# A two-layer transformer on one core: norm weights folded into an output weight, rotary tables made earlier, first loads issued from two queues

## The chip, the core and the metric

One core of one Trainium2 chip runs the whole program. The metric is the device time of one execution in microseconds; a kernel's time is the median of several executions. The engines are TensorE (PE, matmuls), VectorE (DVE), ScalarE (ACT), GpSimd (POOL) and SyncE (SP, which issues most transfers).

## The reference

Two layers over 256 positions of width 1024, all in float32. Layer 0 has a gated linear attention (GLA), layer 1 a block attention with rotary embedding, and each is followed by a gated feed-forward network (FFN). The lines that the change touches:

```python
def rms_norm(x, g, eps=1e-6):
    xf = x.astype(jnp.float32)
    return (xf * lax.rsqrt(jnp.mean(xf * xf, -1, keepdims=True) + eps) * g).astype(x.dtype)

def gla_mixer(x, w_in, w_gk, b_gk, norm_g, w_out):
    q, k, v, g, gk_low = split_cols(x @ w_in, GLA_COLS)
...
    o = from_heads(rms_norm(o.astype(x.dtype), norm_g)) * jax.nn.silu(g)
    return o @ w_out

def partial_rope(x, positions):
    inv_freq = ROPE_THETA ** (-jnp.arange(0, ROPE_DIM, 2, dtype=jnp.float32) / ROPE_DIM)
    ang = positions.astype(jnp.float32)[:, None, :, None] * inv_freq
    cos, sin = jnp.cos(ang), jnp.sin(ang)
...
```

`norm_g` has 256 weights, one for each column of a head; the four heads use the same ones. `cos` and `sin` depend on the positions alone and are first used in layer 1.

## The kernel before

**Products in three passes.** A float32 matrix is split into a rounded part `h` and the rest `l`, both in a format that TensorE runs at full rate, and each product is three matmuls: hh, lh and hl (`mm3`, L291 to L293). So every weight of 128x1024 elements costs an ACT cast (`h`, L263) and a DVE subtraction (`l`, L264) after its 512 KB load; activations are transposed on TensorE (`transpose_split`, L306) and split in the same way (L315 on ACT, L319 on DVE).

**The order is planned when the program is built.** Every step is an `Op` with an engine, a cost from a formula and its reads and writes. `Plan.emit` is a list scheduler: it takes the engine and the step that can start first by these costs, among equals the one created first (steps marked `urgent` may go ahead), and writes the instructions out in that order. Each engine then runs its instructions strictly in that order and waits at each for what it needs. The costs are guesses: for DVE 0.14 us + 0.97 ns for each element of a row, for a load its KB / 330 on SP and 2.3 us more until it lands. Large tiles share 41 slots of 128x1024 elements, given out in order of creation; a load whose slot isn't free yet holds SP.

**The start.** DVE zeroes a tile, and PE multiplies it with itself 7 times (`busy(WARM[0])`, L670; each is two instructions in the trace). SP issues `ident`, the two halves of x's first 128 rows (`x0`), the first two 256 KB pieces of the V weights (`wv00`, `split2`, L273 to L276), the halves of `x1`, then 512 KB pieces of weights. x is transposed into `xT0`; the V product (tile `v`) follows.

**The first attention.** V's first half, the decay chain (`gk`, `pre`, then Abs, Exp, Ln, a scan and three Exp, L728 to L766), K and Q (`gk`, `gq`), scores (`sc`, L819), V's second half, and then for each 128 rows `t`: the attention products (`o`, L862), the sums of squares (L871), the gate product `g` in two blocks with Silu (`sg`, L844), the multiplication of `sg` with `normg` on POOL (L848), and `og`, the product of `o`, the norm factor and `sg` on DVE (L887). `og` is transposed (`trg`, L896) and split (L900, L904), and `out_proj` multiplies it with `gla_w_out` (tile `y`, weights `wo0` to `wo7`).

**The rotary tables** (`rope_tables`, L920 to L950) are created after that projection: three small loads, then 18 DVE instructions on 32x256 elements and two ACT Sin. Their planned costs are 0.637 + 4 x 1.013 + 0.388 = 5.08 us of DVE. They are first used in layer 1. The FFN of layer 0 follows (tiles `fg`, `fu`, `d`, `A`, `X`).

Of the kernel before, what the change touches and what calls it, by code (L numbers as in the profile page):

```python
# [37 lines left out]
WARM = (7, 4)  # L38
# [153 lines left out]
def kernel(ctx, tc, x, positions, gla_w_in, gla_w_gk, gla_b_gk, gla_norm_g, gla_w_out,  # L192
# [30 lines left out]
    normg = fixed("normg", (P, GLA_DV))  # L223
# [60 lines left out]
    def w_row(name, w, k):  # L284
        return split(name, lambda raw: [(raw, w[k * P:(k + 1) * P, :])])
# [634 lines left out]
    def rope_tables():  # L920
        dma(lambda: nc.sync.dma_start(rcol.f, c_f32[:, 2 * P:2 * P + 2]), 4, [], [rcol])
        dma(lambda: nc.sync.dma_start(cmask.f, c_f32[:, P:2 * P]), 64, [], [cmask])
        dma(lambda: nc.sync.dma_start(q32(posb).bitcast(I32), positions[0:1, :].broadcast_to([ROPE, S])), 32,
            [], [posb])

# [187 lines left out]
```

## Time and profile before

| what | value |
|---|---|
| executions timed | 588.75, 591.04, 591.47 us |
| median | 591.04 us |
| the profiled execution, its own time | 588.38 us |
| its span (first to last instruction) | 586.6 us |
| granted TensorE clock, mean | 0.997 |
| PE / PEld / DVE / ACT / POOL busy | 97 / 83 / 86 / 58 / 7% of the span |

The profiled execution lies 1.78 us above its span and 2.66 us under the median. PE's busy time contains the junk matmuls of the start.

### The profile page before, as it was taken

Reading aid. Unit: us, or ns where it says so; the run is one execution under the profiler, and the core shown is the slowest. Engines: PE = TensorE matmul, PEld = TensorE weight load, DVE = VectorE, ACT = ScalarE, POOL = GpSimd, SP = SyncE. Lnnn points to the kernel's source line nnn. Section 1 sums busy time; section 2 is a strip of 40 time slices with the busy share of each in tenths; the row PEclk is TensorE's granted clock in tenths of the full one; section 3 lists DMA queues with packets and bytes.
Section 4 is the critical chain, followed back from the end, with each engine's and each line's share of the span. In section 5 each row is a group of like instructions: output and inputs, shape, how many; then the busy total and the mean of one; then the engine's idle time right before and its main releaser. Section 6 shows DMA issues by size and latency. Waiting matters only on the chain.

```text
span 586.6 us, 8058 instructions
## 1 busy us (share of the span) xinstructions
PE 571.8 (97%) x3006; PEld 488.0 (83%) x3006; DVE 506.3 (86%) x627; ACT 340.1 (58%) x452; POOL 42.8 (7%) x43
## 2 busy tenths in 40 slices
PE   8999998999999999999999999999999999999994
PEld 7899886888878887889889999888887888888983
DVE  4889169988999999999895689988989999999826
ACT  4893455254948586776364356634585767677310
POOL 1022211010010101000000000000101000010001
PEclk9999999999999999999999999999999999999998
DMA  8985176248687878887375545626767888988201
GB/s 267 381 297 166 67 257 208 91 165 232 218 228 231 237 217 284 205 304 251 104 252 187 158 130 188 218 91 215 173 222 226 206 260 204 299 204 275 84 0 72
DMA packets 56233, 118.43 MB, mean 202 GB/s; under 512 B 4945, under 2 KB 9585, under 8 KB 56194
## 3 DMA queue, kind: packets, MB, share of 16 engines
q1 hardware_dynamic: 51842, 109.53, 56.4%
q0 software_dynamic: 4352, 8.39, 8.4%
q8 instruction: 23, 0.38, 0.2%
q14 instruction: 16, 0.13, 0.1%
HBM read 116.85 MB, written 1.05 MB: 201 GB/s over the span
## 4 chain that ended last, share of the span: by engine, by line
PE 83%; DVE 9%; DMA 4%; issue 2%; ACT 0%; SPq 0%; DVEq 0%; ACTq 0%
PE fy L293 6%; PE fy L291 6%; PE fy L292 6%; PE pa L544 4%; PE pa L543 4%; PE pa L541 4%; PE tr L306 3%; PE v L293 3%; PE v L291 3%; PE v L292 3%; DMA d0r<-in_ffn_w_down 2%; PE y L292 2%; PE y L293 2%; PE y L291 2%; PE pc L544 2%; PE pc L543 2%
## 5 line engine op out<-in xcount | busy, mean ns | idle before, releaser
L561 DVE TENSOR_TENSOR A<-A,X 128x1024 f32<-128x1024 f32 x48 | 57.2, 1214 | 0.0
L567 POOL DMA_DIRECT2D X<-in_ffn_w_gu x16 | 19.5, 1236 | 205.5 <-DVE e L595 61.8
L315 ACT CAST xT<-tr 128x512 fp32r<-128x512 f32 x16 | 9.3, 589 | 34.5 <-PE tr L306 34.4
L362 POOL TENSOR_TENSOR st<-st,mhalf 128x1 f32<-128x1 f32 x8 | 7.6, 955 | 252.9 <-DVE st L360 252.9
L499 ACT CAST C0h<-X 128x1024 fp32r<-128x1024 f32 x8 | 8.4, 1053 | 10.9 <-DMA X<-in_ffn_w_gu 10.9
L350 DVE SCALAR_TENSOR_TENSOR r<-xn,fy 128x512 f32<-128x512 f32 x8 | 5.5, 684 | 9.6 <-PE fy L293 9.6
L306 PE MATMUL tr<-ident,e 128*128 128x128 f32 x64 | 9.7, 274 | 2.8 <-DVE e L595 2.7
L306 PEld LDWEIGHTS tr<-ident,e 128*128 128x128 f32 x64 | 7.6, 140 | 5.7 <-issue 4.3
L499 ACT CAST D0h<-A 128x1024 fp32r<-128x1024 f32 x8 | 8.4, 1051 | 6.6 <-DVE A L561 6.6
L499 ACT CAST C1h<-X 128x1024 fp32r<-128x1024 f32 x8 | 8.4, 1051 | 5.9 <-DMA X<-in_ffn_w_gu 5.9
L354 DVE BATCH_NORM_STATS2 st<-r 128x6 f32<-128x512 f32 x16 | 11.1, 693 | 0.5
L319 DVE TENSOR_TENSOR xT<-tr,xT 128x512 fp32r<-128x512 f32 x16 | 10.8, 683 | 0.6 <-ACT x32b L326 0.6
L499 ACT CAST A1h<-A 128x1024 fp32r<-128x1024 f32 x8 | 8.4, 1051 | 5.0 <-DMA A<-in_ffn_w_gu 5.0
L372 DVE SCALAR_TENSOR_TENSOR xn<-r,st,lnb 128x512 f32<-128x512 f32 x16 | 11.3, 745 | 0.0
L499 ACT CAST A0h<-A 128x1024 fp32r<-128x1024 f32 x8 | 8.4, 1055 | 4.8 <-DMA A<-in_ffn_w_gu 4.7
L368 DVE SCALAR_TENSOR_TENSOR r<-r,st,lng 128x512 f32<-128x512 f32 x16 | 11.2, 744 | 0.0
L499 ACT CAST B1h<-A 128x1024 fp32r<-128x1024 f32 x8 | 8.4, 1054 | 3.5 <-DVE A L561 3.3
L499 ACT CAST B0h<-A 128x1024 fp32r<-128x1024 f32 x8 | 8.4, 1050 | 2.7 <-DVE A L561 2.7
L499 ACT CAST G1h<-A 128x1024 fp32r<-128x1024 f32 x8 | 8.4, 1054 | 2.5 <-DVE A L561 2.2
L500 DVE TENSOR_TENSOR G0l<-A,G0h 128x1024 fp32r<-128x1024 f32 x8 | 9.7, 1215 | 0.1
L500 DVE TENSOR_TENSOR E0l<-X,E0h 128x1024 fp32r<-128x1024 f32 x8 | 9.7, 1216 | 0.0
L500 DVE TENSOR_TENSOR D0l<-A,D0h 128x1024 fp32r<-128x1024 f32 x8 | 9.7, 1216 | 0.0
(1034 smaller groups left out, 2269.3 us busy)
## 6 DMA issues: line engine op xcount, KB each, us to landing
X<-in_ffn_w_gu SPq DMA_DIRECT2D x48, 512.0 KB, 5.0
A<-in_ffn_w_gu SPq DMA_DIRECT2D x16, 512.0 KB, 4.3
X<-in_ffn_w_gu POOLq DMA_DIRECT2D x16, 512.0 KB, 8.6
lng<-in_ln_g SPq DMA_DIRECT2D x4, 512.0 KB, 3.6
lnb<-in_ln_b SPq DMA_DIRECT2D x4, 512.0 KB, 5.3
x<-in_x SPq DMA_DIRECT2D x4, 256.0 KB, 4.5
fg00r<-in_ffn_w_gu SPq DMA_DIRECT2D x2, 512.0 KB, 6.5
fg01r<-in_ffn_w_gu SPq DMA_DIRECT2D x2, 512.0 KB, 7.3
```

What stands on the lines that cost most here:

```text
L291: nc.tensor.matmul(ps, lh, rh, start=start, stop=False)
L292: nc.tensor.matmul(ps, ll, rh, start=False, stop=False)
L293: nc.tensor.matmul(ps, lh, rl, start=False, stop=stop)
L306: nc.tensor.transpose(ps.f[:, j * P:(j + 1) * P], src.f[:, k * P:(k + 1) * P], ident.f)
L372: nc.vector.scalar_tensor_tensor(out=xn.f[:, sl], in0=r.f[:, sl], scalar=st.f[:, 15:16], in1=b.f[:, sl], op0=ALU.mult, op1=ALU.add)
L499: act(1024, lambda: nc.scalar.copy(hi.r, raw.f), [raw], [hi])
L500: dve(1024, lambda: nc.vector.tensor_tensor(out=lo.r, in0=raw.f, in1=hi.f, op=ALU.subtract), [raw, hi], [lo])
L541: nc.tensor.matmul(ps.f, sh, wh.r[:, cs], start=first and q == 0 and j == 0, stop=False, skip_group_check=True)
L543: nc.tensor.matmul(ps.f, sl_, wh.r[:, cs], start=False, stop=False, skip_group_check=True)
L544: nc.tensor.matmul(ps.f, sh, wl.r[:, cs], start=False, stop=last_ and q == 1 and j == 1, skip_group_check=True)
L561: dve(1024, lambda q=q, other=other: nc.vector.tensor_tensor(out=raws[q].f, in0=raws[q].f, in1=other.f, op=ALU.add), [raws[q], other], [ra ...
L567: nc.gpsimd.dma_start(uv(raws[q]), unit(kh, gu, q, c0), accum_op=ALU.add)
```

## The change

- The multiplication of `sg` with `normg` on POOL is gone. `normg` is now loaded as two columns of 128 values, and the split of `gla_w_out` multiplies each row by its weight: ACT's cast takes it as a scale, DVE's subtraction becomes a multiply and subtract.
- `rope_tables` is created before the loads of V's second half. Its four tiles take slots there, and its steps come earlier in the order of creation.
- `ident` and the two pieces of `wv00` are issued from ACT; x from SP, with `x0`'s first half first. An empty step of 0.8 us on SP exists in the plan alone.
- `wv00` and `wv01` are loaded in two halves each, and their casts go to ACT instead of DVE. The second junk block has 3 matmuls instead of 4 and stands between the two halves of x0's transposes.

The moved rotary code is the same text in both places and is cut here.

```diff
--- before.py
+++ after.py
@@ -35,7 +35,7 @@
 SLOTS = 41
 BANKS = {"acc": 4, "ps": 4}
 HOLD = {"PE": 0.0, "DVE": 0.5, "ACT": 0.5, "POOL": 0.0, "SP": 0.0}
-WARM = (7, 4)
+WARM = (7, 3)
 
 
 class Buf:
@@ -220,7 +220,7 @@
     cmask = fixed("cmask", (P, P))
     imask = fixed("imask", (P, P), I32)
     rcol = fixed("rcol", (P, 2))
-    normg = fixed("normg", (P, GLA_DV))
+    normg = fixed("normg", (P, GLA_DV // P))
     wgk = fixed("wgk", (GLA_RANK + 1, 512))
     gkT = fixed("gkT", (GLA_RANK + 1, S))
     rope = fixed("rope", (ROPE, 2, S))
@@ -250,7 +250,8 @@
         return pl.op("POOL", 1.3, fn, reads, writes, extra=8.0, **kw)
 
 
-    def split(name, parts, zero=False):
+    def split(name, parts, zero=False, scale=None):
+
         raw, hi, lo = S_(name + "r"), S_(name + "h", True), S_(name + "l", True)
         if zero:
             gps(500, lambda: nc.gpsimd.memset(raw.f, 0.0), [], [raw])
@@ -260,29 +261,38 @@
             for dst, src in parts(raw.f):
                 nc.sync.dma_start(dst, src)
         dma(load, kb, [], [raw])
-        act(1024, lambda: nc.scalar.copy(hi.r, raw.f), [raw], [hi])
-        dve(1024, lambda: nc.vector.tensor_tensor(out=lo.r, in0=raw.f, in1=hi.f, op=ALU.subtract), [raw, hi], [lo])
+        if scale is None:
+            act(1024, lambda: nc.scalar.copy(hi.r, raw.f), [raw], [hi])
+            dve(1024, lambda: nc.vector.tensor_tensor(out=lo.r, in0=raw.f, in1=hi.f, op=ALU.subtract), [raw, hi], [lo])
+        else:
+            act(1024, lambda: nc.scalar.activation(hi.r, raw.f, AF.Copy, scale=scale[1]), [raw, scale[0]], [hi])
+            dve(1024, lambda: nc.vector.scalar_tensor_tensor(out=lo.r, in0=raw.f, scalar=scale[1], in1=hi.f,
+                                                             op0=ALU.mult, op1=ALU.subtract), [raw, hi, scale[0]], [lo])
         return hi, lo
 
-    def split2(name, w, k0, c0):
+    def split2(name, w, k0, c0, act_queue=False):
         raw, hi, lo = S_(name + "r"), S_(name + "h", True), S_(name + "l", True)
         hi.fine = True
         for j in range(2):
             sl = slice(512 * j, 512 * j + 512)
             k = k0 + j
-            dma(lambda sl=sl, k=k: nc.sync.dma_start(raw.f[:, sl], w[k * P:(k + 1) * P, c0:c0 + 512]), 256,
-                [], [(raw, j)])
-            dve(512, lambda sl=sl: nc.vector.tensor_copy(hi.r[:, sl], raw.f[:, sl]), [(raw, j)], [(hi, j)], fast=True, urgent=True, prio=-1)
+            if act_queue:
+                pl.op("ACT", 0.45, lambda sl=sl, k=k: nc.scalar.dma_start(
+                    raw.f[:, sl], w[k * P:(k + 1) * P, c0:c0 + 512]), [], [(raw, j)], extra=3.6 + 1.3 * j, urgent=True)
+            else:
+                dma(lambda sl=sl, k=k: nc.sync.dma_start(raw.f[:, sl], w[k * P:(k + 1) * P, c0:c0 + 512]), 256,
+                    [], [(raw, j)])
+            act(512, lambda sl=sl: nc.scalar.copy(hi.r[:, sl], raw.f[:, sl]), [(raw, j)], [(hi, j)], urgent=True)
             dve(512, lambda sl=sl: nc.vector.tensor_tensor(out=lo.r[:, sl], in0=raw.f[:, sl], in1=hi.f[:, sl],
-                                                           op=ALU.subtract), [(raw, j), (hi, j)], [(lo, j)])
+                                                           op=ALU.subtract), [(raw, j), (hi, j)], [(lo, j)], urgent=True)
         return hi, lo
 
     def w_kcols(name, w, k0, nk, c0, n):
         src = w[k0 * P:(k0 + nk) * P, c0:c0 + n].rearrange("(k p) c -> p k c", p=P)
         return split(name, lambda raw: [(raw.rearrange("p (k c) -> p k c", k=nk), src)])
 
-    def w_row(name, w, k):
-        return split(name, lambda raw: [(raw, w[k * P:(k + 1) * P, :])])
+    def w_row(name, w, k, scale=None):
+        return split(name, lambda raw: [(raw, w[k * P:(k + 1) * P, :])], scale=scale)
 
     def load_cols(name, w, c0):
         return [w_kcols(f"{name}{i}", w, 2 * i, 2, c0, 512) for i in range(KT // 2)]
@@ -416,8 +426,8 @@
         sl = slice(512 * blk, 512 * blk + 512)
         act(512, lambda: nc.scalar.copy(vt[t].f[:, sl], ps.f), [ps], [(vt[t], blk)])
 
-    def out_proj(aT, w, xo, gb, dstT, keep):
-        ws = [w_row(f"wo{k}", w, k) for k in range(KT)]
+    def out_proj(aT, w, xo, gb, dstT, keep, scale=None):
+        ws = [w_row(f"wo{k}", w, k, scale and scale(k)) for k in range(KT)]
         xn = []
         for t in range(2):
             y = [pl.buf("acc", f"y{t}{hf}") for hf in range(2)]
@@ -671,13 +681,12 @@
         return f
     pl.op("PE", 2.9, busy(WARM[0]), [zeros], [junkps])
     xs = [S_("x0"), S_("x1")]
-    dma(lambda: nc.sync.dma_start(ident.f, c_f32[:, 0:P]), 64, [], [ident])
-
-    def load_x(t):
-        for hf in range(2):
-            sl = slice(512 * hf, 512 * hf + 512)
-            dma(lambda xt=xs[t], t=t, sl=sl: nc.sync.dma_start(xt.f[:, sl], x[t * P:(t + 1) * P, sl]), 256,
-                [], [(xs[t], hf)])
+    pl.op("ACT", 0.45, lambda: nc.scalar.dma_start(ident.f, c_f32[:, 0:P]), [], [ident], extra=2.8, urgent=True)
+
+    def load_x(t, hf, extra):
+        sl = slice(512 * hf, 512 * hf + 512)
+        pl.op("SP", 0.78, lambda xt=xs[t]: nc.sync.dma_start(xt.f[:, sl], x[t * P:(t + 1) * P, sl]), [], [(xs[t], hf)],
+              extra=extra)
 
     def keyed(T, fn):
         T.keys = fn
@@ -688,20 +697,23 @@
         return keyed(T, lambda t, k: Tk(T, t, k))
 
     T0 = new_xT("xT0")
-    load_x(0)
-    for hf in range(2):
-        transpose_split(xs[0], T0, 0, hf, skey=hf)
-    pl.op("PE", 1.0, busy(WARM[1]), [zeros, xs[0]], [junkps], urgent=True)
-
+    load_x(0, 0, 2.9)
 
     w0 = gla_w_in[0]
     V0, G0, GK0 = 1024, 2048, 3072
     v_sb = [S_("v0"), S_("v1")]
-    wv0 = [split2("wv00", w0, 0, V0)]
-    load_x(1)
+    wv0 = [split2("wv00", w0, 0, V0, True)]
+    pl.op("SP", 0.8, lambda: None)
+    load_x(0, 1, 2.9)
     for hf in range(2):
+        transpose_split(xs[0], T0, 0, hf, skey=hf)
+        if hf == 0:
+            pl.op("PE", 0.6, busy(WARM[1]), [zeros, (xs[0], 0)], [junkps], urgent=True)
+    for hf in range(2):
+        load_x(1, hf, 2.9)
         transpose_split(xs[1], T0, 1, hf, skey=hf)
-    wv0 += [w_kcols(f"wv0{i}", w0, 2 * i, 2, V0, 512) for i in range(1, KT // 2)]
+    wv0.append(split2("wv01", w0, 2, V0))
+    wv0 += [w_kcols(f"wv0{i}", w0, 2 * i, 2, V0, 512) for i in range(2, KT // 2)]
     vps = [pl.buf("acc", f"v0{t}") for t in range(2)]
     for i in range(KT // 2):
         for t in range(2):
@@ -803,7 +815,8 @@
     gps(350, lambda: nc.gpsimd.tensor_copy(kxv()[:, 1, :, 0:CHUNK], ch(qd, 2)), [qd], [(kx, 3)])
 
     dma(lambda: nc.sync.dma_start(imask.f, c_i32), 64, [], [imask])
-    dma(lambda: nc.sync.dma_start(normg.f, gla_norm_g[0:1, :].broadcast_to([P, GLA_DV])), 128, [], [normg])
+    dma(lambda: nc.sync.dma_start(normg.f, gla_norm_g[0].rearrange("(c p) -> p c", p=P),
+                                  ), 8, [], [normg])
     scs = [S_("sc0"), S_("scx")]
 
     def scv(i):
@@ -830,6 +843,45 @@
     pe(4 * 512, fscx, [kx], [psx])
     act(512, lambda: nc.scalar.copy(scv(2), psx.f.rearrange("p (h c) -> p h c", h=GLA_H)), [psx], [(scs[1], 0)])
 
+
+    posb, ang, kk_, rr_ = S_("posb"), S_("ang"), S_("kk"), S_("rr")
+
+    def q32(b):
+        return b.f[0:ROPE, 0:S]
+
+    def rope_tables():
+        dma(lambda: nc.sync.dma_start(rcol.f, c_f32[:, 2 * P:2 * P + 2]), 4, [], [rcol])
+        dma(lambda: nc.sync.dma_start(cmask.f, c_f32[:, P:2 * P]), 64, [], [cmask])
+        dma(lambda: nc.sync.dma_start(q32(posb).bitcast(I32), positions[0:1, :].broadcast_to([ROPE, S])), 32,
+            [], [posb])
+
...
+    rope_tables()
     wv1 = load_cols("wv1", w0, V0 + 512)
     v_block(1, 0, T0, wv1, v_sb)
 
@@ -842,11 +894,6 @@
         act_block(ps, T0, ws, t)
         sl = slice(512 * blk, 512 * blk + 512)
         act(512, lambda: nc.scalar.activation(sg[t].f[:, sl], ps.f, AF.Silu), [ps], [(sg[t], blk)], table="silu")
-
-        def fg():
-            v3 = sg[t].f[:, sl].rearrange("p (j c) -> p j c", j=2)
-            nc.gpsimd.tensor_tensor(out=v3, in0=v3, in1=normg.f.unsqueeze(1).broadcast_to([P, 2, GLA_DV]), op=ALU.mult)
-        gps(512, fg, [(sg[t], blk), normg], [(sg[t], blk)])
 
     wgs = [load_cols("wg0", w0, G0), load_cols("wg1", w0, G0 + 512)]
     for t in range(2):
@@ -909,49 +956,10 @@
     gb = load_ln(0, 0)
     T1 = new_xT("xT1")
     x32 = [S_("x32a"), S_("x32b")]
-    xs = out_proj(ogT, gla_w_out[0], xs, gb, T1, x32)
-
-
-    posb, ang, kk_, rr_ = S_("posb"), S_("ang"), S_("kk"), S_("rr")
-
-    def q32(b):
-        return b.f[0:ROPE, 0:S]
-
...
+    xs = out_proj(ogT, gla_w_out[0], xs, gb, T1, x32, lambda k: (normg, normg.f[:, k % 2:k % 2 + 1]))
 
     gb = load_ln(0, 1)
     T2 = new_xT("xT2")
-    rope_tables()
     xs = ffn(0, xs, T1, gb, T2, False, x32)
```

## Rows read from the trace of the kernel before

**Rows 1.** Busy time of each engine by stretch; PE, PEld, DVE, ACT, POOL, clock, DMA.

```profile
0.00:4.60 4.60, 3.36 (x15) 3.10 (x15) 0.43 (x3) 1.28 (x1) 2.17 (x7) 1.00 0.50 133
4.60:9.70 5.10, 3.96 (x24) 3.56 (x25) 2.61 (x6) 1.63 (x3) 0.00 (x0) 1.00 0.94 311
9.70:96.90 87.20, 87.20 (x513) 76.81 (x511) 64.17 (x77) 56.66 (x78) 13.49 (x12) 1.00 0.71 246
96.90:99.00 2.10, 0.04 (x1) 0.03 (x1) 2.10 (x4) 0.53 (x1) 0.00 (x0) 1.00 0.00 0
140.00:560.00 420.00, 417.23 (x2176) 355.13 (x2176) 386.03 (x463) 260.45 (x342) 20.69 (x18) 1.00 0.69 208
```

**Rows 2.** Who waited for whom, PE: us in total, times, longest.

```profile
PE tr L306 <- DVE e L595: 2.7, 3, 1.4
PE trg L896 <- DVE og L887: 2.1, 1, 2.1
```

**Rows 3.** Timeline of the start: start, us, what; in brackets the idle time before.

```profile
0.74 0.38 SPq L674 DMA_DIRECT2D ident<-in_c_f  x1
1.18 0.89 SPq L679 DMA_DIRECT2D x<-in_x  x2
3.06 0.91 SPq L679 DMA_DIRECT2D x<-in_x  x2
...
4.60 1.94 PE L306 MATMUL tr<-ident,x 128*128 128x128 f32 x8 [0.18 <-DMA x<-in_x]
...
8.54 1.41 PE L306 MATMUL tr<-ident,x 128*128 128x128 f32 x8 [1.02 <-DMA x<-in_x]
...
9.71 0.48 PE L291 MATMUL v<-wv00h,xT 128*128 128x512 f32 x1
```

**Rows 4.** Instructions of tile x and of tile wv00r: issue to landing.

```profile
DMA to landing us min/median/max: 3.3/4.5/5.6
...
DMA to landing us min/median/max: 5.2/5.2/5.2
```

**Rows 5.** Timeline of the stage of the stall, 87 to 99 us.

```profile
87.66 1.41 DVE L927 CAST ang<-posb 32x256 f32<-32x256 int32 x1 [2.46 <-DMA posb<-in_positions]
...
94.49 0.58 ACT L844 ACTIVATE sg<-g 128x512 f32<-128x512 f32 x1
...
95.15 1.31 POOL L848 TENSOR_TENSOR sg<-sg,normg 128x512 f32<-128x512 f32 x1 [6.23 <-ACT sg L844]
95.26 1.47 DVE L936 SCALAR_TENSOR_TENSOR rr<-kk,ang 32x256 f32<-32x256 f32 x1
...
98.39 0.85 DVE L887 SCALAR_TENSOR_TENSOR og<-o,ss,sg 128x256 f32<-128x256 f32 x2
99.00 0.74 PE L896 MATMUL trg<-ident,og 128*128 128x128 f32 x4 [2.07 <-DVE og L887]
```

**Rows 6.** Instructions of tile kk alone, 82 to 104 us: DVE busy, count.

```profile
82.00:104.00 22.00, 5.20 (x12) 1.00 0.64 217
```

**Rows 7.** Busy time by stretch of the first attention, columns as in rows 1.

```profile
20.00:36.00 16.00, 16.00 (x123) 15.19 (x122) 12.61 (x12) 14.43 (x17) 0.00 (x0) 1.00 1.06 381
36.00:48.00 12.00, 12.00 (x102) 12.00 (x102) 12.00 (x14) 11.15 (x12) 4.94 (x5) 1.00 0.56 194
58.00:68.00 10.00, 10.00 (x46) 8.27 (x45) 0.36 (x2) 5.08 (x12) 2.19 (x2) 1.00 0.17 54
```

**Rows 8.** Timeline before the scores, and the first score matmuls (tile sc, first to last).

```profile
44.32 1.39 POOL L800 COPY kx<-ke 128x256 f32<-128x256 f32 x1
...
49.58 0.68 DVE L781 SCALAR_TENSOR_TENSOR qd<-gq,ep 128x512 f32<-128x512 f32 x1
...
L819 PE MATMUL sc<-qd,ka x16: 217/275/275, 51.5 to 54.7; 128*128 128x64 f32 x16
```

**Rows 9.** Timeline of ACT in the decay chain.

```profile
29.18 1.28 ACT L749 ACT_TABLE_LOAD   x1
30.47 1.06 ACT L749 ACTIVATE la<-la 128x1024 f32<-128x1024 f32 x1
```

More of the change, by code (lines that the diff above doesn't have):

```diff
@@ L831, with f0, f1, f2 @@
     act(512, lambda: nc.scalar.copy(scv(2), psx.f.rearrange("p (h c) -> p h c", h=GLA_H)), [psx], [(scs[1], 0)])
+    posb, ang, kk_, rr_ = S_("posb"), S_("ang"), S_("kk"), S_("rr")
[6 more added lines that the diff above has]
+            [], [posb])
+        def f0():
+            nc.vector.tensor_copy(q32(ang), q32(posb).bitcast(I32))
+            nc.vector.tensor_scalar_mul(q32(ang), q32(ang), rcol.f[0:ROPE, 0:1])
+        dve(512, f0, [posb, rcol], [ang])
+        for which, off in ((0, 0.25), (1, 0.0)):
+            def f1(off=off, which=which):
+                k_, r_, a_ = q32(kk_), q32(rr_), q32(ang)
+                nc.vector.tensor_scalar(out=k_, in0=a_, scalar1=1.0 / TWO_PI, scalar2=off, op0=ALU.mult, op1=ALU.add)
+                nc.vector.tensor_scalar_add(k_, k_, MAGIC)
+                nc.vector.tensor_scalar_add(k_, k_, -MAGIC)
+                nc.vector.scalar_tensor_tensor(out=r_, in0=k_, scalar=-C1, in1=a_, op0=ALU.mult, op1=ALU.add)
+            def f2(which=which):
+                k_, r_ = q32(kk_), q32(rr_)
+                nc.vector.scalar_tensor_tensor(out=r_, in0=k_, scalar=-C2, in1=r_, op0=ALU.mult, op1=ALU.add)
+                nc.vector.scalar_tensor_tensor(out=r_, in0=k_, scalar=-C3, in1=r_, op0=ALU.mult, op1=ALU.add)
+                if which == 0:
+                    nc.vector.tensor_scalar_add(r_, r_, math.pi / 2.0)
+                nc.vector.tensor_scalar(out=r_, in0=r_, scalar1=SIN_MAX, scalar2=-SIN_MAX, op0=ALU.min, op1=ALU.max)
+            dve(900, f1, [ang], [kk_, rr_])
+            dve(900, f2, [kk_, rr_], [rr_])
+            act(256, lambda which=which: nc.scalar.activation(rope.f[:, which, :], q32(rr_), AF.Sin), [rr_],
+                [(rope, which)], table="silu")
+        dve(256, lambda: nc.vector.tensor_scalar_mul(rope.f[:, 1, :], rope.f[:, 1, :], rcol.f[0:ROPE, 1:2]),
+            [(rope, 1), rcol], [(rope, 1)])
+    rope_tables()
     wv1 = load_cols("wv1", w0, V0 + 512)
@@ L911 @@
     x32 = [S_("x32a"), S_("x32b")]
-    xs = out_proj(ogT, gla_w_out[0], xs, gb, T1, x32)
-    posb, ang, kk_, rr_ = S_("posb"), S_("ang"), S_("kk"), S_("rr")
-    def q32(b):
-        return b.f[0:ROPE, 0:S]
[L920 to L924, printed above, removed]
-        def f0():
-            nc.vector.tensor_copy(q32(ang), q32(posb).bitcast(I32))
-            nc.vector.tensor_scalar_mul(q32(ang), q32(ang), rcol.f[0:ROPE, 0:1])
-        dve(512, f0, [posb, rcol], [ang])
-        for which, off in ((0, 0.25), (1, 0.0)):
-            def f1(off=off, which=which):
-                k_, r_, a_ = q32(kk_), q32(rr_), q32(ang)
-                nc.vector.tensor_scalar(out=k_, in0=a_, scalar1=1.0 / TWO_PI, scalar2=off, op0=ALU.mult, op1=ALU.add)
-                nc.vector.tensor_scalar_add(k_, k_, MAGIC)
-                nc.vector.tensor_scalar_add(k_, k_, -MAGIC)
-                nc.vector.scalar_tensor_tensor(out=r_, in0=k_, scalar=-C1, in1=a_, op0=ALU.mult, op1=ALU.add)
-            def f2(which=which):
-                k_, r_ = q32(kk_), q32(rr_)
-                nc.vector.scalar_tensor_tensor(out=r_, in0=k_, scalar=-C2, in1=r_, op0=ALU.mult, op1=ALU.add)
-                nc.vector.scalar_tensor_tensor(out=r_, in0=k_, scalar=-C3, in1=r_, op0=ALU.mult, op1=ALU.add)
-                if which == 0:
-                    nc.vector.tensor_scalar_add(r_, r_, math.pi / 2.0)
-                nc.vector.tensor_scalar(out=r_, in0=r_, scalar1=SIN_MAX, scalar2=-SIN_MAX, op0=ALU.min, op1=ALU.max)
-            dve(900, f1, [ang], [kk_, rr_])
-            dve(900, f2, [kk_, rr_], [rr_])
-            act(256, lambda which=which: nc.scalar.activation(rope.f[:, which, :], q32(rr_), AF.Sin), [rr_],
-                [(rope, which)], table="silu")
-        dve(256, lambda: nc.vector.tensor_scalar_mul(rope.f[:, 1, :], rope.f[:, 1, :], rcol.f[0:ROPE, 1:2]),
-            [(rope, 1), rcol], [(rope, 1)])
```

## The prediction

> **What bounds the kernel now.** I read the table of busy time by stretch first [rows 1]: from 9.70 to 96.90 us TensorE is busy without a break, and from 140 to 560 it lacks 420 - 417.23 = 2.77 us. The span is TensorE's work plus the few places where it has none. Two such places lie where the change works: the start, in which the first useful product begins at 9.71 us [rows 3], and 96.90 to 99.00, in which PE is busy 0.04 of 2.10 us [rows 1]. The list of waits gives that second one its name, 2.1 us for `og` on VectorE, and shows that the only other long PE wait is 2.7 us in three pieces in the FFNs [rows 2]. Cheaper ScalarE or GpSimd work elsewhere is worth nothing; a change is worth what it takes from these holes, less what it opens elsewhere.
>
> **The stall at 97 us.** The timeline shows why `og` is late [rows 5]. VectorE begins the rotary tables at 87.66, and its in-order queue runs them between the splits and `og`. The twelve instructions on `kk` take 5.20 us [rows 6], the cast of the positions 1.41 [rows 5], and five more of the same 32x256 shape some 0.3 each: about 8.1 us. The plan gave the tables 5.08 us. So VectorE runs about 3.0 us behind the plan by which `trg` was placed in PE's queue, and PE pays 2.07 [rows 5]. Part of the 3.0 is one instruction of 1.47 us which runs beside the POOL multiplication of `sg` (95.15 for 1.31 us) [rows 5]; the other eleven on `kk` average (5.20 - 1.47) / 11 = 0.34, so undisturbed it would be about 1.1 shorter, and the tables about 7.0.
>
> The change takes both out of this stage. `sg` is ready at 94.49 + 0.58 = 95.07; without the POOL step `og` needn't wait until 95.15 + 1.31 = 96.46, and without the tables VectorE is 7 to 8 us ahead. `og` could then start right after `sg`, at about 95.1, take 0.85, and `trg` follow at about 96.2, before PE has run out at 96.90; ACT, which also waited for VectorE's sines in front of `sg`, only gets earlier. I take the whole 2.07. Bounds: 0 if a new plan places `trg` just as tightly, 2.07 the whole hole.
>
> **The POOL step and the scaled split.** The four POOL multiplications lie beside full PE work except in that last one, so they give nothing more. The scaled subtraction of `gla_w_out` on DVE is of another kind of instruction (three operands); the nearest rows, 0.68 for `qd` with 512 elements [rows 8] and 0.85 for the two `og` [rows 5], show nothing dearer than a plain subtraction by more than a tenth. Eight times 0.1 to 0.2 is 0.8 to 1.6 us of DVE, and DVE is busy only 0.36 of 10 us from 58 to 68 [rows 7], where most of them run: cost 0. Without that cover it would be late for `y`, at 0.8.
>
> **The start.** PE's order is: transposes of x0, junk, transposes of x1, then `v`. `v` starts at 9.71 because x1's second half came last: the x1 transposes wait 1.02 us for x at 8.54 [rows 3]. SP issues x1 fourth, from 3.06 for 0.91, so its second half at about 3.5; issue to landing is 5.6 at most [rows 4]: 9.1. After the change SP begins with x: x1's second half is the fourth issue on SP instead of the seventh, at 0.74 + 3 x 0.45 = 2.1, 1.4 earlier. But latency grows along the queue, 3.3 to 5.6 us [rows 4], so the bytes wait for the DMA engines, not for the issue; and ahead of x1's last half lie the same bytes as before, since `wv00` now comes from ACT at the same time. On that view only the head of the queue is gained, the 0.44 between `ident` and x (0.74 and 1.18 [rows 3]). So 0.44 to 1.4. From 0 to 4.60 us the DMA share is 0.50 and from 4.60 to 9.70 0.94 at 311 GB/s, against 1.06 at 381 later [rows 1, 7], so there is a little room for a second queue, and I take 0.6. It reaches the end undiminished, since PE has no other break before 96.90.
>
> The Trainium skill speaks against the second queue ("DMA: Bandwidth & Descriptors", section "Issuing engines are not separate DMA queues"): transfers of all issuing engines end on the same 16 DMA engines, and a second issuer saves only the issue time. By it the start gives 0.44 instead of 0.6, and the sum below 2.5 instead of 2.7; the growing latencies agree with it.
>
> `wv00` and `wv01` are cast by ACT (0.59 for 512 columns as in the `sg` row of 0.58 [rows 5]) instead of DVE; ACT is busy 1.63 of 5.10 us then [rows 1], so this is hidden behind x1's landing. If ACT's first table load stood ahead of its issues, `ident` and `wv00` would be issued 1.28 later [rows 9]; `wv00` then at 2.0 + 0.4 = 2.4 lands by 5.2 [rows 4] at 7.6, still before x1: 0. The junk block that is one matmul shorter lies in PE's wait for x, the empty SP step issues nothing, and `normg`, now 256 single values, is needed first by the split of `wo0` after 50 us: 0 each.
>
> **The tables in their new place.** Created before V's second half, they come when their positions land, at 20 to 36 us. VectorE has 16 - 12.61 = 3.39 us free there, and from 36 to 48 none [rows 7]; the rest of 7.0 pushes the splits of `wv1` and `wg` back by 3.6 us, into the free time from 58 to 68 [rows 7]. Queued behind them are `qd` and `kx`, and behind these the scores on PE. The second `qd` ends at 49.58 + 0.68 = 50.26, the scores begin at 51.5 [rows 8]: slack 1.2. The plan's error moves too, 7.0 - 5.08 = 1.9; it costs PE 1.9 - 1.2 = 0.7 if nothing absorbs it and nothing if the 3.39 us free before it do. I take 0, and keep 0 and 2.8 (two more us of wait for a landing that comes late in a full queue) as bounds. Four slots less, SP issues four weight loads later; `wg` has some 10 us in hand (the free stretch [rows 7]): 0, and without that some 1.4 us for each late load (512 KB at 381 GB/s [rows 7]).
>
> **The sum.** 2.07 + 0.6 - 0 = 2.7 us less. Against the profiled execution: span 586.6 - 2.7 = 583.9, and with the 1.78 around it 585.7. That execution lies at the low end: 588.38, and the three runs 588.75, 591.04, 591.47. The mean of the four is 589.9, and I count from there: 589.9 - 2.7 = **587.2**. Less than 0.5% (about 3 us) either way can't be told from no change.
>
> **The rivals.**
> A, the sum as above: 587.2 (586.2 to 588.4).
> B, more is gained: the first product isn't queued behind x1. `wv00`, issued at 1.2, lands by 5.2 [rows 4] at 6.4; cast, subtraction and hand-overs (0.59 + 0.68 + 0.4) make 8.0, so `v` starts 1.7 earlier, not 0.6; and with 7 us less on VectorE ahead of the FFN the longest wait there, 1.4 [rows 2], may go. 2.07 + 1.7 + (0 to 1.4) = 3.8 to 5.2: 584.7 to 586.1. For it: VectorE is behind in that stretch. Against it: the 1.4 comes 70 us later, and the order of PE at the start is x1 first.
> C, the stall moves: VectorE is behind the plan by 2 to 4 us at `qd`, and PE waits 0.7 to 2.8 for the scores. 2.7 - 0.7 = 2.0 to 2.7 - 2.8 = -0.1: 587.9 to 590.0. For it: the mechanism is that of the stall removed, and VectorE is full there.
> D, slower: the Sin stand in ACT's in-order queue amid Exp and Ln, wait for positions and tables, and hold the decay chain, whose last copy on POOL before the scores ends at 44.32 + 1.39 = 45.71, 5.8 ahead of them [rows 8]. It decides from a delay of 5.8 + 2.7 = 8.5 us on. All DVE work of the tables (8.1) and two more table loads of 1.28 [rows 9] make 10.7: PE would wait 4.9, net 2.2 slower, 592.1; with a late landing of another 2 us 594.1. Against it: the chain's steps are urgent and were created first.
> Of the loads the skill says more ("ScalarE: Activation LUTs", section "What ACT_TABLE_LOAD costs"): 2.66 us for a switch, a drain included. The trace shows 1.28 with the next step 0.01 later [rows 9]; by the page D's two loads would be 5.3 and its time 594.8.
>
> **How the numbers follow.** A 0.40, B 0.22, C 0.25, D 0.13. B and about half of A lie more than 0.5% below, with a little of C from the runs' own spread: faster 0.45. Half of A, nearly all of C and a quarter of D are within: same 0.45. The rest of D: slower 0.10. The range reaches from just under B's lower end, 584.3, over C to the first half of D, 591.2, and leaves out D's dearer half and some of the runs' spread; A alone gives 586.2 to 588.4.
>
> **What would show it.** Right: no PE hole between the last `g` and `y`; the rotary instructions among the splits at 25 to 40 us; no POOL work on `sg`; `v` at about 9.1; `sc` follows its neighbours without a gap. Wrong: a PE wait at `sc` on `qd` (C) or on `kb` (D), a hole of 1 us or more at another `trg` or in the FFN from the new order, or `v` at or after 9.7. If `v` starts before the x1 transposes it is B. The clock was granted in full, 1.00, from 4.60 us on [rows 1]; if it isn't when `v` begins, the new place of the junk has cost that.

## The result, and the profile after

The changed kernel takes 586.69 us (median of 9 executions, 585.54 to 589.76) beside 590.73 for the kernel before (9 executions, 588.41 to 592.05): a ratio of 0.9942, 95% interval 0.992 to 0.9963. It is faster by 0.58%, and its time lies 0.5 us from the 587.2 predicted. The gain fits less well: 4.0 us between these medians, 2.7 predicted; the prediction counted from 589.9, and the kernel before took 590.73 here. In the experiments below the changed kernel was timed once more: 0.9958, 0.9939 to 0.9978, a gain of 3.2. The profiled execution after took 585.54 us with a span of 583.8, against 588.38 and 586.6, and this pair has a gain of 2.8. Executions of one kernel differ with the mean granted clock: of 31 of the kernel before (those timed beside the first four experiments), the five at 0.990 to 0.991 took 592.2 to 593.7 us and the eight at 0.997 to 0.998 587.7 to 590.8.

"Lead" below means how much earlier a matmul starts than the same matmul of the kernel before. Read from the two timelines of PE, the lead is 1.65 us at the first `v` (8.06 against 9.71 [rows 3]), 1.70 at the first `sc`, 0.55 at the first `y`, 2.93 at the first matmul of `y` with `wo7`, 3.17 at the first `y` of layer 1, and 2.8 in the span. So the path to 2.8 was not the predicted one: more was won at the start, something was lost again at the scores, and the hole at 97 us gave a little more than was expected. (The list of waits counts from the modelled end of the matmul before; counted in starts, a hole is 0.1 to 0.3 us longer.)

Timeline of the start after the change (start, us, what; in brackets the idle time before it):

```profile
0.74 0.41 ACTq L684 DMA_DIRECT2D ident<-in_c_f  x1
0.74 1.80 SPq L688 DMA_DIRECT2D x<-in_x  x4
1.17 0.93 ACTq L280 DMA_DIRECT2D wv00r<-in_gla_w_in  x2
2.14 1.28 ACT L285 ACT_TABLE_LOAD   x1 [2.14 <-issue]
...
7.67 0.63 PE L316 MATMUL tr<-ident,x 128*128 128x128 f32 x4 [0.32 <-DMA x<-in_x]
...
8.06 0.48 PE L301 MATMUL v<-wv00h,xT 128*128 128x512 f32 x1
```

All four halves of x are now issued by 2.54 us; before, the last went out at about 3.5 [rows 3]. The order on PE is unchanged: `v` still follows the transposes of x1.

Timeline at the scores, and the list of PE's waits:

```profile
49.06 0.67 DVE L793 SCALAR_TENSOR_TENSOR qd<-gq,ep 128x512 f32<-128x512 f32 x1
49.66 1.20 DVE L266 TENSOR_TENSOR wg01l<-wg01r,wg01h 128x1024 fp32r<-128x1024 f32 x1
50.80 0.67 DVE L793 SCALAR_TENSOR_TENSOR qd<-gq,ep 128x512 f32<-128x512 f32 x1
...
51.52 0.43 PE L832 MATMUL sc<-qd,ka 128*128 128x64 f32 x2 [0.63 <-DVE qd L793]
```

```profile
PE tr L316 <- DVE e L605: 2.0, 3, 0.8
...
PE sc L832 <- DVE qd L793: 0.6, 1, 0.6
```

This is a new wait. PE came to the scores 1.70 us earlier, and VectorE finished the second `qd` at 50.80 + 0.67 = 51.47 instead of 50.26 [rows 8]. The matmuls that need it would have begun at about 50.73. Between `sc` and the next V product the lead falls from 1.70 to 0.60, 0.8 of it (from 50.73 to 51.52) at the recorded wait of 0.63. Some 0.2 more goes at the last score product (`scx`, which needs `kx`): it starts at 54.39, right behind POOL's copy into `kx`:

```profile
42.67 6.73 POOL L812 COPY kx<-ke 128x256 f32<-128x256 f32 x1
51.53 2.81 POOL L815 COPY kx<-qd 128x256 f32<-128x256 f32 x1 [2.13 <-DVE qd L793]
```

The second copy ends at 54.34. Before, these two copies took 1.39 [rows 8] and 1.33.

Timeline of the former stall, and busy time from 97 to 99 us (columns as in rows 1):

```profile
93.23 0.58 ACT L896 ACTIVATE sg<-g 128x512 f32<-128x512 f32 x1
...
95.50 0.47 DVE L934 SCALAR_TENSOR_TENSOR og<-o,ss,sg 128x256 f32<-128x256 f32 x1
...
96.22 0.60 PE L943 MATMUL trg<-ident,og 128*128 128x128 f32 x4
```

```profile
97.00:99.00 2.00, 2.00 (x11) 1.59 (x10) 2.00 (x3) 1.79 (x3) 0.00 (x0) 1.00 0.00 0
```

`og` is done in time, `trg` starts with no idle time before it, and PE is busy 2.00 of 2.00 us, where it was busy 0.04 of 2.10 [rows 1, 5].

The tables run where they were expected, from 29.08 on, and ScalarE's part of them shows the additional table loads:

```profile
30.67 1.28 ACT L879 ACT_TABLE_LOAD   x1
32.68 0.42 ACT L879 ACTIVATE rope<-rr 32x256 f32<-32x256 f32 x1 [0.73 <-DVE rr L876]
33.01 1.03 ACT L265 CAST wv10h<-wv10r 128x1024 fp32r<-128x1024 f32 x1
34.05 1.28 ACT L776 ACT_TABLE_LOAD   x1
36.21 1.06 ACT L776 ACTIVATE em<-cum 128x1024 f32<-128x1024 f32 x1 [0.87 <-DVE cum L764]
```

After each of these loads ScalarE still waits for VectorE (0.73 and 0.87 us). PE never waits for the decay chain: rival D did not happen. But D's margin shrank: the copy of `ke` into `kx`, done at 45.71 before [rows 8], is done at 49.40 now.

### The profile page after: what moved, and what is told of

It is laid out like the page before. It is cut to its first block, busy times and chain, and to the rows that moved or that the text cites. A ratio compares the mean times of both kernels' runs of the same rounds, so it can differ in the third digit from the quotient of the medians.

```text
span 583.8 us, 8061 instructions
## 1 busy us (share of the span) xinstructions
PE 571.4 (98%) x3004; PEld 486.9 (83%) x3004; DVE 503.3 (86%) x626; ACT 344.9 (59%) x457; POOL 42.6 (7%) x39
## 4 chain that ended last, share of the span: by engine, by line
PE 74%; DVE 13%; DMA 7%; issue 3%; ACT 1%; DVEq 0%; SPq 0%; ACTq 0%
PE fy L301 6%; PE fy L302 6%; PE fy L303 6%; PE pa L554 3%; PE pa L553 3%; PE pa L551 3%; PE y L302 3%; PE y L303 3%; PE y L301 3%; DMA d0r<-in_ffn_w_down 2%; PE tr L316 2%; PE v L301 2%; DMA wq2r<-in_gla_w_in 2%; PE v L303 2%; PE v L302 2%
## 5 line engine op out<-in xcount | busy, mean ns | idle before, releaser
L934 DVE SCALAR_TENSOR_TENSOR og<-o,ss,sg 128x256 f32<-128x256 f32 x8 | 3.6, 478 | 9.6 <-ACT sg L896 9.6
L510 DVE TENSOR_TENSOR B0l<-A,B0h 128x1024 fp32r<-128x1024 f32 x8 | 9.7, 1214 | 0.8 <-ACT B0h L509 0.8
L510 DVE TENSOR_TENSOR F1l<-X,F1h 128x1024 fp32r<-128x1024 f32 x8 | 9.7, 1216 | 0.0
```

## The experiments

All kernels compute the whole reference. The first four were timed beside a kernel before of 590.31 us, the next four beside 589.60, the last three beside 589.86.

**The start alone.** The new start, with the weights not folded and the tables in their old place.

```diff
-WARM = (7, 4)
+WARM = (7, 3)
...
-    wv0 = [split2("wv00", w0, 0, V0)]
-    load_x(1)
+    wv0 = [split2("wv00", w0, 0, V0, True)]
+    pl.op("SP", 0.8, lambda: None)
+    load_x(0, 1, 2.9)
```

> The kernel before with the new start alone (ident and wv00 issued from ACT, x first on SP, casts of wv00 and wv01 on ACT). Theory 1 (the wait at the scores comes from the rotary work on VectorE ahead of qd): v starts at about 8.1 as in the changed kernel (9.71 before), there is no wait of PE at sc, the lead of 1.65 us reaches trg whole, the stall there stays at about 2.1, span about 585.0. Rival (PE's lead alone brings the wait, since VectorE doesn't get earlier with it): PE waits 0.6 us at sc for qd, the lead is about 0.6 behind it, span about 586.0.

587.91 us, ratio 0.9963 (0.994 to 0.9987). `v` at 8.23, lead 1.48; no wait at `sc`; the lead is 1.53 at the first `y`. The stall stays:

```profile
93.23 1.30 POOL L854 TENSOR_TENSOR sg<-sg,normg 128x512 f32<-128x512 f32 x1 [5.84 <-ACT sg L850]
93.36 1.46 DVE L942 SCALAR_TENSOR_TENSOR rr<-kk,ang 32x256 f32<-32x256 f32 x1
...
97.09 0.74 PE L902 MATMUL trg<-ident,og 128*128 128x128 f32 x4 [1.68 <-DVE og L893]
```

The start is worth some 1.5 us, not 0.6, and alone it causes no wait at the scores. It doesn't cure the stall. In the span only 0.25 is left (586.4, where 585.0 was expected): the lead is 1.92 at `wo7`, 1.66 at the first `y` of layer 1, and 0.46 at its last one, for a reason that the last experiments below show.

**The tables alone.**

```diff
+    rope_tables()
     wv1 = load_cols("wv1", w0, V0 + 512)
...
     T2 = new_xT("xT2")
-    rope_tables()
```

> The kernel before with the rotary tables moved ahead of V's second half, nothing else. Theory 1: PE waits 0.6 to 1.1 us at sc although v starts at 9.7 as before; rival (PE's lead): no wait at sc. On the stall at trg: if the tables made it (as the prediction has it), it is gone, and the span is 586.6 - 2.1 + (0.6 to 1.1) = 585.1 to 585.6; if the POOL step on sg made it, 1 us or more of it stays.

587.06, ratio 0.9937 (0.9914 to 0.996). No wait at `sc`, although the second `qd` is as late as in the changed kernel (50.72): PE is not early here. The stall is gone without the fold: lead 0.11 at the first `y`, 2.49 at `wo7`.

**The fold alone.**

```diff
-        gps(512, fg, [(sg[t], blk), normg], [(sg[t], blk)])
...
-    xs = out_proj(ogT, gla_w_out[0], xs, gb, T1, x32)
+    xs = out_proj(ogT, gla_w_out[0], xs, gb, T1, x32, lambda k: (normg, normg.f[:, k % 2:k % 2 + 1]))
```

> The kernel before with the norm weights folded into gla_w_out alone; no POOL step on sg, tables where they were. If the tables made the stall at trg: VectorE still runs them between splits and og, a stall of 1 us or more stays, span 585.5 or more. If the POOL step made it (1.4 us of hop, and two rotary instructions that ran beside it took 1.41 and 1.47 us, against 0.27 and 0.41 in the changed kernel): the stall is under 0.3, span about 584.5.

586.99, ratio 0.9947 (0.992 to 0.9974). The stall is gone here too, with the tables on VectorE between the last splits:

```profile
87.72 0.28 DVE L929 CAST ang<-posb 32x256 f32<-32x256 int32 x1 [1.51 <-DMA posb<-in_positions]
...
95.26 0.41 DVE L938 SCALAR_TENSOR_TENSOR rr<-kk,ang 32x256 f32<-32x256 f32 x1
95.60 0.86 DVE L890 SCALAR_TENSOR_TENSOR og<-o,ss,sg 128x256 f32<-128x256 f32 x2
...
96.21 0.74 PE L899 MATMUL trg<-ident,og 128*128 128x128 f32 x4
```

The same cast took 1.41 and the same step on `rr` 1.47 beside the POOL multiplication [rows 5]. Without it they take 0.28 and 0.41. So folding removes the hop over POOL and 2.2 us of VectorE as well.

The tables alone, the fold alone and the whole change have a lead of 3.15, 3.13 and 3.17 at the first `y` of layer 1 (the tables 2.35 and the whole 3.38 in a second profile), and ratios of 0.9937, 0.9947 and 0.9942 (0.9954 and 0.9958 when timed again). That the whole is faster than either of these parts is not shown.

**One queue.** The changed kernel, with `ident` and `wv00` issued from SP.

```diff
-    pl.op("ACT", 0.45, lambda: nc.scalar.dma_start(ident.f, c_f32[:, 0:P]), [], [ident], extra=2.8, urgent=True)
+    dma(lambda: nc.sync.dma_start(ident.f, c_f32[:, 0:P]), 64, [], [ident])
...
-    wv0 = [split2("wv00", w0, 0, V0, True)]
+    wv0 = [split2("wv00", w0, 0, V0)]
```

> The changed kernel with ident and wv00 issued from SP again, one queue for all; casts, order of the pieces and everything else as changed. Theory 2 (the second queue moves more bytes in the first microseconds, 395 GB/s against 311): v starts at 9.2 or later, span 1.1 us or more above the changed kernel's 583.8. Rival 2 (a second queue saves issue time alone): v at about 8.5, span about 584.2. Rival 3 (order and casts did it): v at about 8.1.

586.33, ratio 0.9946 (0.9923 to 0.9969). The planner put the first `v` ahead of the transposes of x1 here, so its start (6.25) can't be compared; at `gk` the lead is 1.0 instead of 1.7. There is no wait at `sc`: PE comes 0.7 us later, and the plan placed the second `qd` right behind the first (both done by 49.94). A plan changes with its inputs, so this run doesn't isolate the queue in time. What it does show is the landing: the last half of x is issued at 3.54 and lands at 8.66, against 7.54 in the changed kernel.

**The second queue alone.** The kernel before, with only these issues moved to ACT.

```diff
-    dma(lambda: nc.sync.dma_start(ident.f, c_f32[:, 0:P]), 64, [], [ident])
+    pl.op("ACT", 0.45, lambda: nc.scalar.dma_start(ident.f, c_f32[:, 0:P]), [], [ident], extra=2.8, urgent=True)
...
-    wv0 = [split2("wv00", w0, 0, V0)]
+    wv0 = [split2("wv00", w0, 0, V0, True)]
```

> The kernel before with one thing changed: ident and the two pieces of wv00 are issued from ScalarE, so x's four halves stand first on SP. Theory 1 (two issuing engines keep more descriptors in flight early, and the transfers run faster): 370 GB/s or more from 4.60 to 9.70 us (311 before), v starts at 8.0 to 8.4. Rule of the second queue saving issue time alone: 311 to 330 GB/s, v starts at 9.2 to 9.4, that is 0.3 to 0.5 earlier. Rival (the order counts, x ahead of wv00 in the queue, not the rate): rate as before but v starts at 8.0 to 8.6, and wv00 lands later. The end: the stall at trg stays and absorbs some of it, span 584.9 to 586.4.

588.60, ratio 0.9992 (0.9973 to 1.001). `v` starts at 8.24: this alone is the whole gain of the start, 1.47. (In the eight profiles with two queues `v` starts between 8.06 and 8.44, in the four with the old start between 9.53 and 9.78.) Instructions of tile `x` and the stretch from 4.60 us (columns as in rows 1):

```profile
L683 SPq DMA_DIRECT2D x<-in_x x4: 382/420/432, 0.7 to 2.1; - x4
DMA to landing us min/median/max: 3.3/4.8/5.6
```

```profile
4.60:9.70 5.10, 4.63 (x31) 3.77 (x29) 3.89 (x8) 2.94 (x5) 0.00 (x0) 1.00 1.04 385
```

The last half of x lands 5.6 us after its issue, as before [rows 4], and the issue itself is at 2.1 instead of 3.5. In size the gain is the issue time of the three pieces that no longer stand ahead of it on SP. But the same bytes also move faster: 385 GB/s against 311 [rows 1]. The numbers that were expected if two queues move the bytes faster came out (370 or more, `v` at 8.0 to 8.4), and those of issue time alone did not (311 to 330, 9.2 to 9.4). Nor is it the order alone: the second piece of `wv00` lands no later for x going first, at 7.31 against 7.75. Window 3 to 7 us of the kernel before, of the run called one queue, and of this kernel:

```profile
3.00:7.00 4.00, 3.82 (x20) 3.55 (x20) 0.00 (x0) 1.01 (x2) 0.00 (x0) 1.00 0.86 233
3.00:7.00 4.00, 3.43 (x18) 2.73 (x17) 1.25 (x2) 1.72 (x3) 0.00 (x0) 1.00 1.02 292
3.00:7.00 4.00, 3.87 (x24) 3.31 (x24) 1.19 (x3) 1.60 (x3) 0.00 (x0) 1.00 1.02 373
```

The five profiles with one queue have 233 to 292 GB/s there, the eight with two queues 359 to 382. It wasn't for want of issued work: by 4.6 us the kernel before had issued some 2.1 MB and moved 0.6 (133 GB/s for 4.60 us [rows 1]). Why one queue moves less here was not tried.

None of it reached the end. The stall stayed, and behind it the clock fell (windows 95 to 98 and 98 to 101):

```profile
95.00:98.00 3.00, 0.93 (x6) 0.40 (x5) 3.00 (x6) 1.01 (x2) 0.02 (x1) 0.95 0.00 0
98.00:101.00 3.00, 3.00 (x10) 2.42 (x10) 2.58 (x5) 1.83 (x3) 0.00 (x0) 0.50 0.39 96
```

At 0.50, the 1.2 GHz level, the `y` matmuls follow each other every 0.43 us instead of 0.23. The lead of 1.43 is 0.64 at `wo7` and 0.08 at the first `y` of layer 1, and the span is 0.4 longer than that of the kernel before.

**Start and fold.** The changed kernel, with the tables in their old place.

```diff
-    rope_tables()
     wv1 = load_cols("wv1", w0, V0 + 512)
...
     T2 = new_xT("xT2")
+    rope_tables()
```

> The new start and the folded weights, with the rotary tables at their old place after the first projection. Theory 1 (the wait at the scores needs both TensorE's lead from the new start and the tables on VectorE ahead of qd): no wait at sc, the lead of 1.5 to 1.7 us is kept from v to the gate product; the stall at trg stays away, since the fold alone removed it; TensorE is 3.5 to 3.8 us ahead of the kernel before at the last trg, and the span is 583.0 or less if the feed-forward network keeps that. Theory 2 (whatever the first attention gives beyond some 3 us is taken back by waits in the first feed-forward network, whose loads and splits have their own pace): the same lead at trg, but TensorE's waits there grow by 0.5 to 0.8 and the span is 583.5 to 584.0, no better than the whole change. Rival: the tables behind the last trg bring part of the stall back with a larger lead, 0.5 to 1.5 us at trg.

586.48, ratio 0.9962 (0.9935 to 0.9988). No wait at `sc` (the tables aren't ahead of `qd`), lead 1.40 at the first `y`; but part of the stall is back, and at `wo7` the lead is 2.22:

```profile
PE trg L905 <- DVE og L896: 1.3, 1, 1.3
```

`trg` starts at 96.09 here and at 96.21 with the fold alone: the tables set that time whether PE is early or not. So moving them is what lets the start's gain pass this place, and the old place costs it there.

**The tables after the scores.** The changed kernel, with the tables created where VectorE has little to do [rows 7, 58 to 68 us].

```diff
         if t == 1:
+            posb, ang, kk_, rr_ = S_("posb"), S_("ang"), S_("kk"), S_("rr")
+            rope_tables()
             v_block(1, 1, T0, wv1, v_sb)
...
-    rope_tables()
     wv1 = load_cols("wv1", w0, V0 + 512)
```

> The whole change, but the rotary tables are created later, with the second half of the attention, so that VectorE computes them after the scores, where it is nearly idle (58 to 68 us). Theory 1: no wait at sc (0.6 in the changed kernel), lead of 1.5 to 1.7 kept through sc, no stall at trg, lead 3.5 to 3.8 after it. The span is 583.0 if the feed-forward network keeps the lead, by theory 2 583.5 to 584.0. Rival (the wait at the scores comes from the two extra table loads of ScalarE in the decay chain, or from a late load, and not from VectorE's tables): if from a late load, a wait of 0.5 or more at sc stays.

585.58, ratio 0.9943 (0.9923 to 0.9962). Both waits are gone. The lead is 1.39 at `sc`, 1.37 at the first `y`, 3.75 at `wo7` and 4.04 at the first `y` of layer 1, so the FFN takes nothing back, and theory 2 falls. Yet the span is 584.6, longer than that of the changed kernel: the lead is 2.48 at the last `wo7` of layer 1. Timelines of ACT and PE in between:

```profile
368.57 1.05 ACT L265 CAST fg00h<-fg00r 128x1024 fp32r<-128x1024 f32 x1 [5.35 <-DVE mst L1022]
...
370.82 0.36 ACT L1027 ACTIVATE pr<-ms,mst 128x128 f32<-128x128 f32 x1
...
372.39 0.61 PE L1043 MATMUL pt<-ident,pr 128*128 128x128 f32 x3 [0.90 <-DVE pr L1034]
```

ScalarE's cast of the FFN weight `fg00` stands in its queue ahead of the Exp of the block attention. The load was issued at 360.1 and landed 8.4 us later; Exp, then VectorE, then PE waited.

**The tables alone, again.** The same kernel, no edit.

> The kernel that only moves the tables, run again. In its first profile the load fg00r in layer 1 landed 8.4 us after its issue (6.5 with the fold alone, issued at the same time), and ScalarE's cast of it held the Exp behind it, so that TensorE lost 1.5 us between 366 and 386 us. If the landing differs from one execution to the next: another value between 6.4 and 8.4, and the lead of 3.1 us at mq reaches the end for a span of 583.7 to 584.8 when it is under 7. If it follows from this kernel's order of transfers: 8.2 to 8.6 again and a span of 585.4 to 586.0.

586.57, ratio 0.9954 (0.9935 to 0.9972). `fg00r` landed 7.4 us after its issue (8.4 in the first profile), and 0.65 us were lost in layer 1 instead of 1.55. So the landing isn't fixed by the kernel. The span was not shorter for it (586.2): the lead was 0.6 smaller at `wo7` of layer 0, and PE waited 1.17 for `e` at 510 us.

**The changed kernel, and the tables after the scores, again.** No edits.

> The changed kernel again, on one chip with the two that follow. If single profiles differ by where the load fg00r lands: the wait of 0.6 us at sc as before, the lead at the first y of layer 1 again 3.0 to 3.3, and a span between 583.5 and 585 that follows the landing of fg00r (6.9 us after issue in the first profile). Time ratio to the kernel before 0.993 to 0.996.

> The kernel with the tables after the scores, again, beside the changed kernel on one chip. If it is worth what its lead of 4.0 against 3.2 at the first y of layer 1 says: 0.8 us, a time ratio 0.001 to 0.002 lower than that of the changed kernel. If landings in layer 1 decide: fg00r lands at another time than in its first profile (8.4 us after issue), and where it lands under 7 us there is no wait at pt and a span of 583.0 or less; the ratio is then the same as the changed kernel's within the interval.

Changed: 586.69, ratio 0.9958 (0.9939 to 0.9978), wait at `sc` 0.40, landing 8.2, span 584.5. Tables after the scores: 584.66, ratio 0.9927 (0.9902 to 0.9953), landing 7.4, span 582.9, 1.7 less than in its first profile. The intervals overlap, though the second median is 2.0 us lower on the same chip. Its larger lead at the first `y` of layer 1 (4.04 and 4.78 against 3.17 and 3.38 in the four profiles) accounts for about 1 us; the rest was not separated.

**The casts later in the plan.** The kernel with the tables after the scores; the loads `fg00` and `fg01` of layer 1 are planned to land later.

```diff
-        dma(load, kb, [], [raw])
+        pl.op("SP", kb / 330.0, load, [], [raw], extra=6.5 if late and name in ("fg00", "fg01") else 2.3)
...
+    late.append(1)
     ffn(1, xs, T3, gb, None, True, x32)
```

> The kernel with the tables after the scores, and one planned number more: the loads fg00 and fg01 of layer 1 are planned to land 6.5 us after their transfer instead of 2.3, so that their casts on ScalarE come behind the Exp of the block attention. If the 1.5 us that TensorE lost between 370 and 384 us came from those casts waiting for their loads: no wait at pt, the lead of 4.0 at the first y of layer 1 is still there at its last, whenever fg00r lands, and the span is 582.3 to 583.3 (0.9 to 1.5 under the kernel without this). Rival (the feed-forward network of layer 1 has its own pace and takes it back, as the wait of 0.9 at 509 suggests): no wait at pt, but 0.5 to 1.5 more in the waits for e, and a span of 583.5 to 584.6.

584.47, ratio 0.9922 (0.9899 to 0.9944), span 582.7. Timelines of ACT and PE, and the landing of `fg00r`:

```profile
368.53 0.37 ACT L1029 ACTIVATE pr<-ms,mst 128x128 f32<-128x128 f32 x1 [5.46 <-DVE mst L1024]
...
370.80 1.07 ACT L267 CAST fg00h<-fg00r 128x1024 fp32r<-128x1024 f32 x1
...
371.18 0.49 PE L1045 MATMUL pt<-ident,pr 128*128 128x128 f32 x3
```

```profile
DMA to landing us min/median/max: 8.5/8.5/8.5
```

The landing was the latest of all, and PE waited for nothing there. It is the fastest version measured, 2.2 us under the changed kernel on the same chip (586.69), but only 0.2 under the same kernel without this edit (584.66), which the intervals don't tell apart: in the profile the loss is gone, in the time a gain from it is not shown. The FFN of layer 1 takes 0.4 us of the lead back: 4.23 at the last matmul of `y`, 3.87 in the span, about as without the edit (4.23 and 3.73), so the rival falls.

The profiles together show the mechanism. Lead lost between the first and the last matmul of `y` in layer 1, in order of the landing of `fg00r`:

| kernel | issue to landing, us | lead lost, us |
|---|---|---|
| fold alone | 6.5 | 0.02 |
| changed | 6.9 | 0.06 |
| one queue | 6.9 | 0.13 |
| second queue alone | 7.1 | 0.23 |
| tables late, again | 7.4 | 0.56 |
| tables alone, again | 7.4 | 0.65 |
| start and fold | 7.7 | 0.94 |
| start alone | 8.0 | 1.20 |
| changed, again | 8.2 | 1.31 |
| tables alone | 8.4 | 1.55 |
| tables late | 8.4 | 1.56 |
| casts later | 8.5 | none |

Down to the last row but one, each microsecond above 6.9 costs one; the profile of the kernel before, at 6.8, is the zero. With the casts behind the Exp, in one profile, the latest landing cost nothing. In the three kernels that were profiled twice `fg00r` landed 0.9 to 1.3 us apart, so single spans of one kernel can differ by as much.

## Why the prediction was right, step by step

**The stall at 97 us: right.** 2.07 predicted; 2.93 - 0.55 = 2.4 between the first `y` and `wo7`. The prediction named two causes, the tables and the POOL step, and taking away either is enough as long as PE comes no earlier (2.49 - 0.11 = 2.4 with the tables moved, 2.2 with the fold). It put the undisturbed tables at 7.0 us on VectorE; they take 5.95 with the fold alone and 6.13 in the changed kernel, because the cast of the positions was stretched by POOL too, which the prediction priced at its full 1.41.

**The start: the size was wrong.** The step that failed is "latency grows along the queue, so the bytes wait for the DMA engines, not for the issue", with "a little room for a second queue". It led to 0.6, near the lower bound, and the gain was above the upper one of 1.4: 1.65, and 1.47 with the queue alone. The bytes did wait, 5.4 to 5.6 us from issue to landing as before; but the DMA engines were not at their limit, for from 3 to 7 us they moved 233 GB/s with one queue and 373 with two. The prediction read windows that cut this stretch at 4.60 us, where the room shows less (311 GB/s at a share of 0.94).

The Trainium skill ("DMA: Bandwidth & Descriptors", section "Issuing engines are not separate DMA queues") says that a second issuer saves issue time only. Counted as all pieces that leave SP's queue ahead of x (three of some 0.45 us), and not only `ident`, as the prediction did for its 0.44, that time is 1.4 and has the size of the gain. The trace does not agree with "only": the rate rose too, in every profile with two queues.

**The tables' new place: 0 taken, about 1.1 paid.** This is rival C towards its cheap end (0.7). The prediction gave `qd` a slack of 1.2 us and let the plan's error of 1.9 be absorbed. Measured, `qd` came 1.2 later, and that alone would have cost nothing (tables alone: no wait). It left out that the start's gain brings PE to the scores earlier by 1.7: the two terms were summed as if they had nothing to do with each other, and "it reaches the end undiminished" failed here. Neither the start nor the tables alone makes PE wait there; together they do (0.63 and 0.40 in the two profiles of the changed kernel).

**The costs taken as nothing: right.** The scaled subtraction takes 1.27 to 1.28 us against 1.22 for the plain one and nothing waits for it; ScalarE has six table loads up to 105 us instead of four, each 1.28, none on PE's path. The clock was full when `v` began.

**The sum: right by luck, through two errors that cancel.** 2.07 + 0.6 - 0 = 2.7 was predicted. Measured up to `wo7`: 1.65 - 1.1 + 2.4 = 2.9, and 2.8 in the span. Rival B had the size of the start (1.7) for a reason that did not hold, since `v` still follows the transposes of x1; C was right on the scores, A on the stall. Of the FFN's waits for `e` (2.7 [rows 2]), 2.2 remain.

**What stays open.** What the first FFN does to the lead differs from profile to profile, from 0.6 us lost to 1.0 added, also for one kernel (0.2 and 0.5 added for the changed one). Why the medians differ by 3.2 to 4.0 us where the profiles' spans differ by 2.1 to 2.8 was not separated; the granted clock of the single executions has a part in it. Why `fg00r` lands 6.9 us after its issue in one execution and 8.2 in the next was not tried.

## What to carry to other kernels

Two gains on one path don't add where the first brings an engine earlier to a place whose other input the second makes later: check each place where a moved step meets the lead that another edit creates. When latency grows along a queue, that alone doesn't say that the DMA engines are the limit: subtract the issue times ahead of the transfer, and look at the rate while the transfers wait. In a planned order, look for an in-order engine that waits for a load ahead of work on the path, and plan the load's landing by what the trace shows; one number took away a loss of up to 1.6 us in the profile, though no gain in the median of these few executions is shown.

## What the runs showed of the hardware

- A small VectorE instruction (32x256 elements) that begins while POOL multiplies `sg` ends only behind it. In the kernel before, the cast took 1.41 us and the step on `rr` 1.47 instead of 0.28 and 0.41, and the latter ended at 96.73, 0.27 after POOL (96.46 [rows 5]). With the start alone the cast began 0.15 us ahead of POOL and took 0.28; the next instruction, normally 0.34, took 1.27. A larger one, the 128x512 subtraction for `ogT` (one input from PSUM), began 0.43 us into POOL's step at 72.27 in the kernel before and took its usual 0.69. The Trainium skill ("SBUF — State Buffer", section "Who interferes with whom") has a rule for this: VectorE and GpSimd share one pair of SBUF ports, which a VectorE instruction uses if it has two inputs in SBUF or runs in a two-port mode; whoever is first holds it for the whole instruction, and the other is blocked. The trace agrees where it can be seen: the six stretched instructions (in three kernels) began 0.03 to 0.17 us behind POOL's and ended 0.1 to 0.3 after it, and the subtraction with a single SBUF input was not stretched. Of the six, the three steps on `rr` have two inputs in SBUF; the other three have one, and no row shows in which mode they ran. With the tables alone VectorE was first: its subtraction for `fg02` (128x1024, both inputs in SBUF) began 0.54 us ahead of POOL's step on `sg` and took its usual 1.22, and POOL's took 1.84 instead of 1.30.
- POOL can wait much longer than that. Its copy of 128x256 elements into `kx` took 6.73 us in the five profiles that have the tables ahead of V's second half, where VectorE ran the tables and then splits beside it, and 1.39 in the kernel before; the same kind of copy into `kb` took 0.40 at its quickest. (Spans on POOL are rough, but `scx` started right behind the second one.) Why POOL got in sooner beside the splits of the kernel before was not tried.
- A hole of 2.07 us on PE left the clock at 1.00 in the kernel before, and one of the same length was followed by 0.50 for some three microseconds in the kernel with the second queue alone, which cost what that kernel had gained; holes of 1.68 (the start alone) and 1.25 (start and fold) left it at 1.00. What decides it was not tried.
